# One layout for the whole kernel in place of six contiguous blocks: how tokens are dealt to partitions in a streaming weighted copy

## The chip, the cores and the metric

The kernel runs on one core of a Trainium2 chip. The metric is the device time of one execution in microseconds; for the kernel before it is 241.01 us, the median of three runs (240.65 to 241.06). A profiled execution gives the span and the trace that the rest of this text reads. Its span, 238.8 us, is a little shorter than the device time of the same execution, 240.52 us.

## The reference

Each token's row of 512 numbers is copied twice, once for each of its two experts, and each copy is multiplied by that expert's weight. The expert indices do not enter the result.

```python
batch, seq, hidden, n_experts, k = 16, 1024, 512, 8, 2
x_expanded = x[:, :, np.newaxis, :].repeat(k, axis=2)
weights = expert_weights[..., np.newaxis]
return (x_expanded * weights).astype(np.float32)
```

There are 16,384 tokens. The input x is 33.55 MB (2 KB a token), the weights are 0.13 MB (8 B a token) and the output is 67.11 MB (4 KB a token). All are float32.

## The kernel before

A tile has 128 partitions, and each partition holds a number of consecutive tokens. With 16,384 tokens a partition sees 128 tokens in all (`A_TOTAL`). The list `groups` says how they are dealt out. An inner list is one group: a stretch of the input that is contiguous in memory, 128 x T tokens for a group of T, where partition p takes T consecutive tokens of the stretch. The numbers in an inner list are the tiles into which the group is cut.

```python
TX = 24     # tokens per partition in an input tile
TO = 12     # tokens per partition in an output tile
groups = [[24], [24], [24], [24], [24], [8]]

def rows(of_all, done, T):
    return of_all[done * P : (done + T) * P, :].rearrange(
        "(p a) n -> p (a n)", a=T
    )
```

So in a group of 24 the tokens of partition p begin 24 tokens after those of partition p-1. That is 48 KB in x and 96 KB in the output.

The weights are loaded first, with one DMA for each group on SyncE's queue. In a group of 24 every partition receives a row of 24 x 2 x 4 = 192 B, in the last group one of 64 B.

```python
for at, T in weights:
    nc.sync.dma_start(out=w_tile[:, at * k : (at + T) * k], in_=rows(wf, at, T))
```

The inputs are loaded on ScalarE's queue. There are two input buffers, and a tile is loaded two tiles ahead of its use. A tile of 24 tokens is one DMA of 6 MB with 128 rows of 48 KB.

```python
def load(i):
    ...
    cols = rows(xf, done, T)[:, a0 * hidden : (a0 + n) * hidden]
    ...
        nc.scalar.dma_start(out=x_tile[lo:hi, : n * hidden], in_=cols[lo:hi, :])
```

The loop multiplies token by token. Of three products VectorE makes two and ScalarE one. After 12 tokens the output tile, again 128 rows of 48 KB, is stored on SyncE's queue. There are two output buffers.

```python
for i, (done, T, a0, n) in enumerate(tiles):
    x_tile = loaded[i]
    outr = rows(of, done, T)
    for t in range(n):
        ...                                   # a new o_tile every TO tokens
        for kk in range(k):
            c = (done + a0 + t) * k + kk
            ...                               # c % 3 == 2: nc.scalar.mul
                                              # otherwise:  nc.vector.tensor_scalar
        if (t + 1) % TO == 0 or t + 1 == n:
            at = t // TO * TO
            nc.sync.dma_start(
                out=outr[:, (a0 + at) * row : (a0 + t + 1) * row],
                in_=o_tile[:, : (t + 1 - at) * row],
            )
    load(i + 2)
```

Of the kernel before, what the change touches and what calls it, by code (L numbers as in the profile page):

```python
# [1 line left out]

# [4 lines left out]


@with_exitstack
def kernel(  # L10
    ctx: ExitStack,
    tc: tile.TileContext,
    x: bass.AP,
    expert_indices: bass.AP,
    expert_weights: bass.AP,
    out: bass.AP,
):
    nc = tc.nc

    batch, seq, hidden = x.shape  # L20
    k = expert_weights.shape[-1]
    P = nc.NUM_PARTITIONS
    ntok = batch * seq
    assert ntok % P == 0
    A_TOTAL = ntok // P

    f32 = mybir.dt.float32
    row = k * hidden
    TX = 24
    TO = 12  # L30


    groups = [[24], [24], [24], [24], [24], [8]]
    assert sum(sum(g) for g in groups) == A_TOTAL

    xf = x.rearrange("b s h -> (b s) h")
    of = out.rearrange("b s k h -> (b s) (k h)")
    wf = expert_weights.rearrange("b s k -> (b s) k")

    w_pool = ctx.enter_context(tc.tile_pool(name="w_pool", bufs=1))  # L40
    x_pool = ctx.enter_context(tc.tile_pool(name="x_pool", bufs=2))
    o_pool = ctx.enter_context(tc.tile_pool(name="o_pool", bufs=2))

    w_tile = w_pool.tile([P, A_TOTAL * k], f32)
# [6 lines that stand above are left out]
    weights = []  # L51
    for group in groups:
        weights.append((sum(n for _, n in weights), sum(group)))
    for at, T in weights:
        nc.sync.dma_start(out=w_tile[:, at * k : (at + T) * k], in_=rows(wf, at, T))

    tiles = []
    done = 0
    for group in groups:
        T = sum(group)  # L60
        a0 = 0
        for n in group:
            tiles.append((done, T, a0, n))
            a0 += n
        done += T

    loaded = []

    def load(i):
        if i >= len(tiles):  # L70
            return
        done, T, a0, n = tiles[i]
        x_tile = x_pool.tile([P, TX * hidden], f32)
        cols = rows(xf, done, T)[:, a0 * hidden : (a0 + n) * hidden]
        for lo, hi in [(0, P)]:
            nc.scalar.dma_start(out=x_tile[lo:hi, : n * hidden], in_=cols[lo:hi, :])
        loaded.append(x_tile)

    for i in range(2):
        load(i)  # L80
# [4 lines that stand above are left out]
            if t % TO == 0:  # L85
                o_tile = o_pool.tile([P, TO * row], f32)
            for kk in range(k):
                c = (done + a0 + t) * k + kk
                o = t % TO * row + kk * hidden
                if c % 3 == 2:  # L90
                    nc.scalar.mul(  # L91
                        out=o_tile[:, o : o + hidden],
                        in_=x_tile[:, t * hidden : (t + 1) * hidden],
                        mul=w_tile[:, c : c + 1],
                    )
                    continue
                nc.vector.tensor_scalar(  # L97
                    out=o_tile[:, o : o + hidden],
                    in0=x_tile[:, t * hidden : (t + 1) * hidden],
                    scalar1=w_tile[:, c : c + 1],  # L100
                    scalar2=None,
                    op0=mybir.AluOpType.mult,
# [9 lines that stand above are left out]
# [1 line left out]
_INS = ['x', 'expert_indices', 'expert_weights']  # L113
_OUTS = [((16, 1024, 2, 512), 'float32')]


# [23 lines left out]
```

## Time and profile before

| quantity | value |
|---|---|
| device time, median of three | 241.01 us |
| span of the profiled execution | 238.8 us |
| VectorE busy | 68.6 us, 171 products of 480 ns |
| ScalarE busy | 54.5 us, 85 products of 709 ns |
| moved by the DMA engines | 100.81 MB, 422 GB/s over the span |
| transfers of x | 5 of 6144 KB, 1 of 2048 KB |
| transfers of the output | 10 of 6144 KB, 1 of 4096 KB |
| transfers of weights | 5 of 24 KB, 1 of 8 KB |

The profile counts busy time of each engine in the span. A core has 16 DMA engines that work side by side; the share of a DMA queue is the time that its packets took as a share of the time of all 16. A packet is here one row of a transfer (one partition's part), or one 4 B word that reports an engine's part of a transfer as done. A wait is put down to the instruction or transfer that ended it.

### The profile page before, as it was taken

To read this page: it belongs to the slowest core of one execution; us is meant where nothing else is said; L and a number is where in the kernel's file an instruction comes from. 1 tells how busy PE (TensorE), PEld (TensorE's weight loads), DVE (VectorE), ACT (ScalarE), POOL (GpSimd) and SP (SyncE) were. 2 spreads that over 40 slices of the span, in tenths; PEclk is the share of its full clock that TensorE was granted. 3 is DMA by queue.
4 is the path that set the end of the run, shared out by engine and by line. 5 is a ranking of instruction groups with operands and counts; after the bars stand their busy time and mean duration, and the time that the engine had idled before them with its cause. 6 is when DMAs were issued, how large, how long until landed. Compare 5 with 4: busy or idle time off the path is not lost.

```text
span 238.8 us, 363 instructions
## 1 busy us (share of the span) xinstructions
DVE 68.6 (29%) x171; ACT 54.5 (23%) x86; POOL 0.2 (0%) x4
## 2 busy tenths in 40 slices
DVE  0009920000270820550054055002705506415000
ACT  0109700000350800520052043003505206213000
POOL 0000000000000000000000000000000000000000
DMA  7999999999999999999999999999989899999994
GB/s 275 462 438 413 421 375 403 477 428 403 445 461 412 413 477 412 412 477 428 412 428 461 420 412 471 428 403 436 469 379 488 384 450 461 436 395 436 439 434 209
DMA packets 3314, 100.81 MB, mean 422 GB/s; under 512 B 1136, under 2 KB 1136, under 8 KB 1136
## 3 DMA queue, kind: packets, MB, share of 16 engines
q1 hardware_dynamic: 2448, 67.24, 65.2%
q10 hardware_dynamic: 864, 33.55, 33.2%
q14 instruction: 2, 0.02, 0.0%
HBM read 33.69 MB, written 67.11 MB: 422 GB/s over the span
## 4 chain that ended last, share of the span: by engine, by line
DMA 60%; DVE 17%; issue 14%; DVEq 0%; SPq 0%
DMA out_dram<-o_tile 53%; DVE o_tile L97 17%; DMA x_tile<-in_x_dram 7%; DVEq L135 0%; DVEq L97 0%; SPq L106 0%
## 5 line engine op out<-in xcount | busy, mean ns | idle before, releaser
L97 DVE TENSOR_SCALAR o_tile<-x_tile,w_tile 128x512 f32<-128x512 f32 x171 | 68.6, 480 | 149.7 <-DMA out_dram<-o_tile 98.5
L91 ACT ACTIVATE o_tile<-x_tile,w_tile 128x512 f32<-128x512 f32 x85 | 53.2, 709 | 151.4 <-DMA out_dram<-o_tile 145.4
L91 ACT ACT_TABLE_LOAD x1 | 1.3, 1283 | 11.2 <-DMA w_tile<-in_expert_weights_dram 11.2
L124 POOL MEMSET const-bfloat16-1.0<- 128x1 bf16 x1 | 0.1, 101 | 0.0
L124 POOL MEMSET const-uint8-127<- 128x1 uint8 x1 | 0.1, 101 | 0.0
L124 POOL MEMSET const-float32-0.0<- 128x1 f32 x1 | 0.1, 98 | 0.2 <-issue 0.2
L124 POOL MEMSET const-float32-1.0<- 128x1 f32 x1 | 0.1, 98 | 0.0
## 6 DMA issues: line engine op xcount, KB each, us to landing
out_dram<-o_tile SPq DMA_DIRECT2D x10, 6144.0 KB, 35.2
x_tile<-in_x_dram ACTq DMA_DIRECT2D x5, 6144.0 KB, 33.3
out_dram<-o_tile SPq DMA_DIRECT2D x1, 4096.0 KB, 19.5
x_tile<-in_x_dram ACTq DMA_DIRECT2D x1, 2048.0 KB, 24.0
w_tile<-in_expert_weights_dram SPq DMA_DIRECT2D x5, 24.0 KB, 32.0
w_tile<-in_expert_weights_dram SPq DMA_DIRECT2D x1, 8.0 KB, 31.5
```

The source lines that it names most:

```text
L91: nc.scalar.mul(out=o_tile[:, o : o + hidden], in_=x_tile[:, t * hidden : (t + 1) * hidden], mul=w_tile[:, c : c + 1],)
L97: nc.vector.tensor_scalar(out=o_tile[:, o : o + hidden], in0=x_tile[:, t * hidden : (t + 1) * hidden], scalar1=w_tile[:, c : c + 1], scala ...
L124: nc = _bacc.Bacc("TRN2", target_bir_lowering=False, num_devices=1)
```

## The change

The six groups become one group of 128 tokens, cut into the same six tiles.

```diff
--- before.py
+++ after.py
@@ -30,7 +30,7 @@
     TO = 12
 
 
-    groups = [[24], [24], [24], [24], [24], [8]]
+    groups = [[24, 24, 24, 24, 24, 8]]
     assert sum(sum(g) for g in groups) == A_TOTAL
 
     xf = x.rearrange("b s h -> (b s) h")
```

Partition p now owns tokens 128p to 128p+127 for the whole kernel. The tiles, their sizes, the buffers, the order and the number of products stay as they are. What differs is where the rows of a transfer lie in memory. Neighbouring rows of an x tile are 128 x 2 KB = 256 KB apart, where before they followed each other without a gap at 48 KB. Neighbouring rows of an output tile are 128 x 4 KB = 512 KB apart, where before they were 96 KB apart. Each row is still one contiguous run of 48 KB (in the last tile 16 KB of x and 32 KB of output). The weights become one DMA with 128 rows of 1 KB. The change makes the code simpler: one weight load, and a fixed owner for each token.

## The prediction on record

> **What bounds the kernel now.** I first read busy times against the span, then the slices, then the DMA queues, then the waits.
>
> ```profile
> span 238.8 us, 363 instructions
> DVE 68.6 (29%) x171; ACT 54.5 (23%) x86; POOL 0.2 (0%) x4
> ...
> DMA  7999999999999999999999999999989899999994
> ...
> q1 hardware_dynamic: 2448, 67.24, 65.2%
> q10 hardware_dynamic: 864, 33.55, 33.2%
> ```
>
> The two engines that compute are idle for over 70% of the span. The DMA engines are at 9 tenths or more in all but four of the 40 slices, the first and last among those four. The queue that carries weights and outputs (q1) takes 65.2% of the 16 engines' time and the one that carries x (q10) 33.2%, together 98.4%. That is 0.984 x 238.8 = 235.0 us of work on each DMA engine, with 3.8 us left, most of it at the two ends. The waits agree:
>
> ```profile
> ACT o_tile L91 <- DMA out_dram<-o_tile: 145.4, 9, 35.5
> DVE o_tile L97 <- DMA out_dram<-o_tile: 98.5, 8, 19.0
> ...
> DVE o_tile L97 <- DMA x_tile<-in_x_dram: 18.4, 1, 18.4
> ACT L91 <- DMA w_tile<-in_expert_weights_dram: 11.2, 1, 11.2
> ACT o_tile L91 <- DMA x_tile<-in_x_dram: 6.0, 1, 6.0
> ```
>
> The columns are total wait, number of waits and longest wait. Compute waits mainly for stores to free an output buffer. A wait for weights occurs once, at 11.2 us, and ends 7 us before the first x tile lands (18.4 us), so it sets nothing. The kernel is bound by the DMA engines through nearly its whole length: a nanosecond more for each row goes straight into the time, and a faster engine elsewhere is worth nothing.
>
> **Whether the memory or the DMA engines set the pace of a row.** In the records of single packets in the trace, the shortest and the median 48 KB row both took 1815 ns, for x and for outputs, which is 27.1 GB/s for one engine and 433 GB/s for 16. Such a sharp floor says that the DMA engine sets the pace and that memory now has some room. Of the 1920 rows of 48 KB only 57 took over 1830 ns. Most of those lie in two bursts of x rows: one at the start, where the first row on each engine took about 1.8 to 2.9 us, and one 29 us into the span, just after the first store is issued, where 16 rows took 2.4 to 3.3 us. The excess of all x rows over 1815 ns is 26.5 us, or 1.7 us per engine. When engines change what they do at the same moment, memory can become the slower side even with today's addresses.
>
> **What the Trainium skill says.** "DMA: Bandwidth & Descriptors", section "Latency and other measured facts", has an entry on row pitch at large powers of two: copies between tensors in HBM, 128 partitions of 16 KiB, at a pitch of 512 KiB gave 207 GB/s in each direction, at 2 MiB 164, at 4 and 8 MiB 103, and 214 with 4 KiB of padding. It calls the cause, rows in step falling on the same HBM channels, an inference. The trace before cannot confirm it: its pitches are 48 and 96 KB, and it runs at the floor. The section "The descriptor swizzle" of the same page deals a 128-partition transfer out to the engines in runs of four partitions (0 to 3 and 32 to 35 for the first). The trace does not name the engine of a packet, so no run here shows it. "Queues, rings and completion order" says that an engine takes packets in turn from the queues that have work for it. Here the trace agrees: at the start a 192 B weight row and a 48 KB x row follow each other on alternate queues, with starts about 12 ns apart.
>
> **The change, part by part.**
>
> *Weights.* Before: 640 rows of 192 B, 15 ns each in the median, and 128 rows of 64 B at 11 ns. Their recorded sum is 9.58 + 1.41 = 10.99 us, or 0.69 us on each of 16 engines. After: 128 rows of 1 KB, 8 per engine. A 48 KB row costs 1815/48 = 37.8 ns per KB; a 192 B row took 15 ns where that rate gives 7.1, so I add 8 ns per row and estimate 46 ns. That is 8 x 46 = 0.37 us per engine. Five transfers fewer also drop five completion words of 9 ns each per engine, 0.05 us. Gain: 0.69 - 0.37 + 0.05 = 0.37 us. All of it is engine time, so it counts in full.
>
> *Start.* The first weight transfer before needed 8 rows per engine and landed at about 11 us, taking turns with x. The new one also has 8 rows per engine, each 31 ns longer, so it should land at about the same moment, well before x at 18.4 us. The SyncE queue issues one transfer instead of six (3.4 us before), off the path. I count zero.
>
> *Compute.* The index c runs over the same numbers, so the split of products is the same, at 480 and 709 ns. Zero.
>
> *Sizes, buffers, tail.* Rows, transfers and order of x and outputs are the same. The last store is again 4 MB. Zero.
>
> *Addresses.* This is the only large term and its sign can only be against the change, because rows already run at the engine's floor for nearly all of the span. Output rows, at 512 KB pitch, take 2324.6 + 155.3 = 2479.9 us, or 155.0 us per engine. X rows, at 256 KB, take 1188.1 + 78.2 = 1266.3 us, or 79.1 us per engine. The page's 214 against 207 is 3.4% more time. If it held for output rows alone, 155.0 x 0.034 = 5.3 us. For both kinds, 234.1 x 0.034 = 8.0 us. But these are loads and stores between HBM and SBUF, where only one end of a row can collide, with rows three times as long, and x has half the pitch of the page's mildest case. Reads and writes are also mixed and out of step, which spreads addresses. I take about 40% of the 5.3 us plus a little for x and starts: 2.4 us.
>
> Sum: 241.0 - 0.4 + 2.4 = 243.0 us.
>
> **The rivals.**
>
> *No penalty.* Memory has enough room, the rows stay at 1815 ns and only the weight gain is left: 241.0 - 0.4 = 240.6 us. For it: the sharp floor at 1815 ns, long contiguous rows, and rows on different engines that start up to about 1 us apart, so that they stand at different offsets. Against it: the bursts above show that memory's room is not unlimited. I give this 40%.
>
> *A mild penalty,* from a fifth of the page's 3.4% up to the whole of it on both kinds: 242 to 248.6 us. For it: the page's 512 KiB figure at a total HBM traffic (2 x 207 = 414 GB/s) very like ours (422 GB/s). Against it: the differences just named. 40%.
>
> *A heavy penalty,* from 249 us up. If engines keep in step and each has a run of four partitions, as the swizzle has it, rows in flight at once are 4 x 512 KB = 2 MB apart in the output and 1 MB in x. The page's 2 MiB figure would then be the one to use: 155.0 x (214/164 - 1) = 47 us for outputs alone, 288 us in all, more with x. For it: engines in this trace do stay within about one row of each other. Against it: the page's pitch is that of partitions, so its 512 KiB case probably contains a similar multiplication already and still lost only 3%. Rows could also collide like this for a part of the time. 18%, half of it below 262 us.
>
> *A gain of over 2%,* which needs 4.8 us. The gaps are 3.8 us and the slow x rows 1.7 us; nearly all of both would have to go, and nothing in the change aims at them. 2%.
>
> **Range and chances.** The lower end is the weight gain plus a part of the slow x rows: 241.0 - 0.4 - 0.6 = 240.0 us. The upper end, 262 us, lies above the whole mild penalty and holds the weaker half of the heavy one. The limit for slower by over 2% is 245.8 us. I put three fifths of the mild 40% below it (24%) and two fifths above (16%). So within 2% is 40 + 24 = 64%, slower is 16 + 18 = 34%, and faster keeps its 2%. The middle of the distribution is near 242.5 us, and I name the sum, 243.0 us.
>
> **What would show each step right or wrong.** Weights: one transfer with 128 rows of 1 KB near 46 ns, and q1 with 720 packets fewer (640 rows and 80 completion words). Start: first product near 18.4 us; later means that the first x tile already suffers. Compute: still 480 and 709 ns with 171 and 85 products. Addresses: the number to look at is the time of a 48 KB row, against 1815 ns, separately for x and outputs. At 1815 ns the first rival is right; up to about 1880 ns the mild one; over 2200 ns on outputs the heavy one. If only a few engines' rows are slow, the DMA share falls while others wait, and median time from issue to landing rises above 35.2 us without the median row doing so. The prediction is wrong if the time falls below 240 us, which would mean that the power-of-two pitches help, or if it exceeds 262 us.

## The result and the profile after

The changed kernel takes 242.19 us (median of six runs, 241.54 to 242.67) against 241.03 us for the kernel before (six runs, 240.65 to 241.17). The ratio is 1.0051, with a 95% interval of 1.0034 to 1.0068: slower by about half a per cent, 1.2 us. The single profiled executions are 2.2 us apart (spans of 241.0 and 238.8 us), so a trace of one execution shows the kind of the loss, and the medians its size.

This is the page of the changed kernel, the lines that answer to those of before:

```profile
span 241.0 us, 358 instructions
DVE 68.6 (28%) x171; ACT 54.5 (23%) x86; POOL 0.2 (0%) x4
...
DMA  7999999999999999999999999999999999999994
...
q1 hardware_dynamic: 1728, 67.24, 64.6%
q10 hardware_dynamic: 864, 33.55, 33.5%
...
out_dram<-o_tile SPq DMA_DIRECT2D x10, 6144.0 KB, 34.3
...
w_tile<-in_expert_weights_dram SPq DMA_DIRECT2D x1, 128.0 KB, 12.0
```

In the last two lines the final number is the median time from issue to landing in microseconds. Compute is the same to the tenth of a microsecond. The DMA engines are just as full, and q1 carries 720 packets fewer. But 64.6% + 33.5% of 241.0 us is 236.4 us of work, against 235.0 us, although the same data is moved with fewer packets. The share of q10 (x) rises while that of q1 falls: rows of x take longer. The waits of the changed kernel:

```profile
ACT o_tile L91 <- DMA out_dram<-o_tile: 147.6, 9, 32.1
DVE o_tile L97 <- DMA out_dram<-o_tile: 133.5, 9, 29.3
DVE o_tile L97 <- DMA x_tile<-in_x_dram: 18.2, 1, 18.2
ACT L91 <- DMA w_tile<-in_expert_weights_dram: 12.8, 1, 12.8
ACT o_tile L91 <- DMA x_tile<-in_x_dram: 4.1, 1, 4.1
```

The start is not worse. The weights arrive at 12.8 us rather than 11.2, still well before the first x tile, and that tile lands at 18.2 rather than 18.4 us. VectorE's wait for stores looks longer (133.5 against 98.5 us), but this is mostly book-keeping. In the kernel before, one more wait of that engine is listed under "issue", that is, with no releaser found:

```profile
DVE o_tile L97 <- issue: 32.8, 1, 32.8
```

With it the two sums are 133.5 and 131.3 us. Compute is idle in either case.

The end of the run shows a second part of the loss. These are the last stretches of before and after: stretch, its length, busy time of the three engines, clock, DMA share, GB/s.

```profile
230.00:235.00 5.00, 0.00 (x0) 0.00 (x0) 0.00 (x0) 1.00 1.05 452
235.00:239.00 4.00, 0.00 (x0) 0.00 (x0) 0.00 (x0) 1.00 0.23 98
```

```profile
230.00:235.00 5.00, 0.00 (x0) 0.00 (x0) 0.00 (x0) 1.00 1.03 446
235.00:241.00 6.00, 0.00 (x0) 0.00 (x0) 0.00 (x0) 1.00 0.39 169
```

After 235 us the mean engine still had 0.23 x 4 = 0.9 us of work before the change, and 0.39 x 6 = 2.3 us after it. A share of 0.39 over several microseconds is not 16 engines at work to the end: most are done and a few finish late. The records of single packets put numbers on both parts. An engine's last packet is the word that reports its part of the last store; times here count from the first data packet of the run, and excess is the time that 48 KB rows took beyond 1815 ns each, summed and divided by 16.

| profiled execution | mean end of the 16 engines | last end | last minus mean | excess, x | excess, output |
|---|---|---|---|---|---|
| before | 234.74 | 235.79 | 1.04 | 1.66 | 0.09 |
| after | 236.18 | 237.74 | 1.56 | 3.05 | 0.32 |

The last engine ends 1.95 us later: 1.44 us because the engines have more work on average, and 0.52 us because the work is spread less evenly. Of the first part, 1.3 us is accounted for: 1.39 + 0.23 us of longer rows, less about 0.3 us for the smaller weight packets. The median row is still 1815 ns. What has changed is how many rows stand out: 98 of 640 rows of x took over 1830 ns (41 before), and 45 of 1280 output rows (16 before). They come in bursts. The burst between 25 and 33 us of the span, where the first store meets the second load of x, grew from 0.97 to 1.59 us per engine, while the slow rows of the first 5 us fell from 0.64 to 0.36 us. New bursts of x rows stand at 41 us (0.32 us) and 57 us (0.50 us), and one of output rows at 132 us (0.21 us).

### The profile page after: what moved, and what is told of

Same layout as the page of the kernel before. It is cut to its first block, busy times and chain, and to the rows that moved or that the text cites. A ratio compares the mean times of both kernels' runs of the same rounds, so it can differ in the third digit from the quotient of the medians.

```text
span 241.0 us, 358 instructions
## 1 busy us (share of the span) xinstructions
DVE 68.6 (28%) x171; ACT 54.5 (23%) x86; POOL 0.2 (0%) x4
## 3 DMA queue, kind: packets, MB, share of 16 engines
q1 hardware_dynamic: 1728, 67.24, 64.6%
q10 hardware_dynamic: 864, 33.55, 33.5%
## 4 chain that ended last, share of the span: by engine, by line
DMA 75%; DVE 15%; issue 0%; DVEq 0%; SPq 0%
DMA out_dram<-o_tile 68%; DVE o_tile L97 15%; DMA x_tile<-in_x_dram 7%; DVEq L135 0%; DVEq L97 0%; SPq L106 0%
## 5 line engine op out<-in xcount | busy, mean ns | idle before, releaser
L97 DVE TENSOR_SCALAR o_tile<-x_tile,w_tile 128x512 f32<-128x512 f32 x171 | 68.6, 480 | 151.7 <-DMA out_dram<-o_tile 133.5
L91 ACT ACT_TABLE_LOAD x1 | 1.3, 1283 | 12.8 <-DMA w_tile<-in_expert_weights_dram 12.8
## 6 DMA issues: line engine op xcount, KB each, us to landing
out_dram<-o_tile SPq DMA_DIRECT2D x10, 6144.0 KB, 34.3
```

The costliest lines, as they stand in the source:

```text
L91: nc.scalar.mul(out=o_tile[:, o : o + hidden], in_=x_tile[:, t * hidden : (t + 1) * hidden], mul=w_tile[:, c : c + 1],)
L97: nc.vector.tensor_scalar(out=o_tile[:, o : o + hidden], in0=x_tile[:, t * hidden : (t + 1) * hidden], scalar1=w_tile[:, c : c + 1], scala ...
```

## The experiments

My theory: rows far apart at a power of two slow each other, x above all, since its excess grew most. Rivals: the output's pitch is the cause and x rows are its victims; mere spreading is enough, without a power of two; the new weight load disturbs the rows. All changes are made to the kernel before unless another is named, and each ratio is to the kernel before as it was timed beside them (240.83 us, and 241.12 us for the stores and loads alone).

**The weight load alone.**

```diff
-    for at, T in weights:
-        nc.sync.dma_start(out=w_tile[:, at * k : (at + T) * k], in_=rows(wf, at, T))
+    nc.sync.dma_start(out=w_tile, in_=rows(wf, 0, A_TOTAL))
```

> The layout of x and of the output as before; only the six weight loads become one of 128 rows of 1 KB (products then use other tokens' weights). If the weights are a small gain that the addresses outweigh, 0.3 to 0.4 us less than before (ratio 0.998 to 0.999) and few slow x rows (about 41 over 1830 ns, excess near 1.7 us per engine). If the new weight load itself disturbs the x rows, 1 us more than before, with x rows slow as in the changed kernel (98 over 1830 ns).

Measured: 240.64 us, ratio 0.9986 (0.9979 to 0.9994), a gain of 0.3 us. 30 rows of x were over 1830 ns, with 1.08 us of excess. The weight load is a small gain, and it does not disturb the rows. The gain did not come as forecast, though: in this trace the 128 weight packets took 16.7 us together, against 11.0 us for the 768 packets before. What fell is the excess of x rows, by 0.58 us per engine.

**The pitch of x alone.**

```diff
-        cols = rows(xf, done, T)[:, a0 * hidden : (a0 + n) * hidden]
+        cols = rows(xf, 0, A_TOTAL)[:, (done + a0) * hidden : (done + a0 + n) * hidden]
```

> Only x is read with rows 256 KB apart; weights are loaded and outputs are stored as before (products land in other tokens' places). If the 256 KB pitch of x is the cause, about 1.5 us more than before (ratio 1.006) and x rows with about 3 us of excess per engine. If the 512 KB pitch of the output is the cause and x rows are only its victims, as before (ratio 1.000) with 1.7 us of excess.

Measured: 241.19 us, ratio 1.0015 (1.0003 to 1.0027), excess of x rows 1.58 us. My theory in its first form falls: reading x at 256 KB makes by itself the smaller part of the loss, 0.4 us and by the interval at most 0.65 us. Nor is it nothing: 7 of its 22 runs took over 241.5 us, against 3 of 51 of the kernel before, and in its trace the last engine ended 2.02 us after the mean, where before it was 1.04 us.

**The pitch of the output alone.**

```diff
-        outr = rows(of, done, T)
+        outr = rows(of, 0, A_TOTAL)[:, done * row :]
```

> Only the output is stored with rows 512 KB apart; x and weights are loaded as before (products land in other tokens' places). If the pitch of x is the cause, as before (ratio 1.000), with 1.7 us of excess on x rows. If the output's pitch is the cause, about 1.5 us more (ratio 1.006).

Measured: 242.43 us, ratio 1.0055 (1.0038 to 1.0072). This change alone makes a loss as large as that of the whole change. Its page and the end of its run:

```profile
span 242.0 us, 363 instructions
...
q1 hardware_dynamic: 2448, 67.24, 64.7%
q10 hardware_dynamic: 864, 33.55, 33.1%
```

```profile
230.00:235.00 5.00, 0.00 (x0) 0.00 (x0) 0.00 (x0) 1.00 0.99 426
235.00:242.00 7.00, 0.00 (x0) 0.00 (x0) 0.00 (x0) 1.00 0.35 150
```

After 235 us there are 0.35 x 7 = 2.5 us of work for the mean engine, at a third of the full share. The packet records give a mean end of 236.18 us and a last end of 238.90, so 2.72 us of unevenness against 1.04 before. This was the slowest of the kernel's six runs (243.63 us), so the end shown is worse than its usual one. The excess is 2.54 us on x rows and 0.54 us on output rows. So although only the store addresses changed, the loads slow down as well, by 0.88 us of the 1.39 us seen in the changed kernel. X rows are to a large part victims, and the share of q10 in the changed kernel had pointed at the wrong transfer.

**Nearly the same spread, without the power of two.**

```diff
-    groups = [[24], [24], [24], [24], [24], [8]]
+    groups = [[24, 24, 24, 24, 24], [8]]
```

> The groups are 24 x 5 tokens and 8 tokens: rows of x 240 KB and of the output 480 KB apart in the first five tiles, nearly as far as in the changed kernel but no power of two; two weight loads. If power-of-two pitches collide, 0.3 us less than before (ratio 0.998 to 0.999), x rows as before. If it is the mere spread over all of x and the output, 1 us more than before (ratio 1.005).

Measured: 240.85 us, ratio 0.9997 (0.9989 to 1.0004). The loss is gone, though rows of the output still lie 480 KB apart. The gain of 0.3 us that I had expected from fewer weight loads is not seen either. The same for the output alone:

```diff
-        outr = rows(of, done, T)
+        outr = rows(of, 0, 120)[:, done * row :] if done < 120 else rows(of, 120, 8)
```

> As the run with the output's rows 512 KB apart, but 480 KB apart in the first ten stores and 32 KB in the last; x and weights as before (products land in other tokens' places). If the exact power of two in the output's pitch matters once loads and stores meet, the time of before (ratio 1.000, within 0.3 us). If wide spreading of stores is enough, the ratio of the 512 KB run, 1.0055.

Measured: 240.71 us, ratio 0.9998 (0.9987 to 1.0008), where 512 KB gave 1.0055. The end of its run is that of the kernel before:

```profile
230.00:235.00 5.00, 0.00 (x0) 0.00 (x0) 0.00 (x0) 1.00 1.00 433
235.00:239.00 4.00, 0.00 (x0) 0.00 (x0) 0.00 (x0) 1.00 0.29 123
```

So spreading alone is not the cause: the loss appears between 480 and 512 KB. The two kernels without it also have contiguous rows in the last store, but that is not the difference, since these 32 KB rows took 1213 ns on average in all of these traces. That 512 KB costs because it is a power of two is the nearest reading and is not shown: no larger pitch was run.

The bursts draw the same line. Leave out the first 31 us after the first packet. Then the x rows of the two kernels so far with the output at 512 KB have 1.09 and 0.94 us of excess per engine and their output rows 0.31 and 0.54 us. In the five others, the kernel before among them, x rows have 0.00 to 0.14 us and output rows 0.05 to 0.13 us.

**Stores alone and loads alone.** Two kernels make the eleven stores from one tile that is filled once; they read no input and multiply nothing. Two others make the six loads and a store of 256 KB at the end. "Far" has the layout of the changed kernel.

```diff
+    o_tile = o_pool.tile([P, TO * row], f32)
+    nc.vector.memset(o_tile, 1.0)
     for i, (done, T, a0, n) in enumerate(tiles):
-        ...
+        outr = rows(of, done, T)                           # near
+        outr = rows(of, 0, A_TOTAL)[:, done * row :]       # far
+        for at in range(0, n, TO):
+            m = min(TO, n - at)
+            nc.sync.dma_start(out=outr[:, (a0 + at) * row : (a0 + at + m) * row],
+                              in_=o_tile[:, : m * row])
```

> The eleven stores alone, from one tile filled once, with rows 96 KB apart as before; no input is read and nothing is multiplied. All theories: 155 us of rows at the floor and about 5 us of start and end, near 160 us.

> The same eleven stores with rows 512 KB apart. If stores collide among themselves in steady flow, rows are over 1815 ns throughout: 162 us or more (the mild penalty in full would be 165 us, the heavy one 200 us or more). If rows collide only where loads and stores meet, the same as with rows 96 KB apart to within 0.5 us.

> The six loads of x alone with rows 48 KB apart, into two buffers in turn; one store of 256 KB at the end, nothing multiplied. All theories: 77.5 us of rows at the floor and about 6 us of start and end, near 84 us.

> The same six loads with rows 256 KB apart. If loads at this pitch collide among themselves, 1 us or more above the loads at 48 KB, with rows over 1815 ns throughout. If the pitch of x does next to nothing by itself, within 0.5 us of them.

Measured: stores 173.04 us near (173.03 to 173.05) and 173.05 us far (173.05 to 173.09). Loads 86.02 us near and 85.60 us far, ratios 0.3568 (0.3558 to 0.3579) and 0.3552 (0.3545 to 0.3558). The stores take 13 us more than I expected, mainly because filling the tile stands ahead of them. This is the far store kernel, start, length, and what ran:

```profile
3.36 10.30 DVE L64 MEMSET o_tile<- 128x12288 f32 x1 [3.36 <-issue]
13.69 6.98 SPq L69 DMA_DIRECT2D out_dram<-o_tile  x7
```

The queues of the near store kernel and then of the far one show the same share of the same span:

```profile
span 171.3 us, 57 instructions
...
q1 hardware_dynamic: 1584, 67.11, 90.9%
```

```profile
span 171.3 us, 57 instructions
...
q1 hardware_dynamic: 1584, 67.11, 90.8%
```

At 512 KB the store rows had a median of 1820 ns, as at 96 KB, with 121 rows over 1830 ns in both. So the pitch costs nothing while only stores run, and loads at 256 KB were even 0.4 us quicker. The loss needs both directions in flight, or the stopping and starting of the whole kernel, which the store runs also lack: there the transfers queue up and wait for no buffer. These runs do not tell the two apart.

**Half the pitch.** Two groups of 64 tokens give pitches of 128 and 256 KB; the second kernel has the same tile sizes in contiguous groups.

```diff
-    groups = [[24], [24], [24], [24], [24], [8]]
+    groups = [[24, 24, 16], [24, 24, 16]]              # 128 and 256 KB
+    groups = [[24], [24], [16], [24], [24], [16]]      # contiguous
```

> Two groups of 64 tokens in tiles of 24, 24 and 16: rows of x 128 KB and of the output 256 KB apart, half the changed kernel's. To be compared with the run of the same tiles and contiguous groups. If any large power of two in the output's pitch costs, 0.5 us or more above that run. If it takes the full 512 KB, the same within 0.3 us, or a little less for two weight loads instead of six.

> Six contiguous groups of 24, 24, 16, 24, 24 and 16 tokens: the tile sizes of the run with pitches of 128 and 256 KB, with the layout of before. One store more than before (twelve). All theories: within 0.5 us of before.

Measured: 241.68 us, ratio 1.0026 (1.0009 to 1.0043), for 128 and 256 KB; 242.23 us, ratio 1.0061 (1.0046 to 1.0075), for contiguous groups. Half the pitch costs nothing against its partner and is even faster; two weight loads in place of six may be part of that. But the partner itself missed its expectation by 0.9 us, and against the kernel before, with its other tile sizes, half the pitch loses 0.6 us. So this pair does not settle whether 256 KB between output rows costs something. In the partner's trace the 256 rows of 32 KB of x took 1275 ns on average against a median of 1213, which makes 1.0 us per engine. The cause is open. It is a reminder that a kernel with no far pitch can lose as much to bursts as the changed one. A loss of about 1 us is thus no mark of the pitch by itself; the case against 512 KB rests on several kernels on each side of it.

**The changed kernel with six weight loads.**

```diff
-    groups = [[24], [24], [24], [24], [24], [8]]
+    groups = [[24, 24, 24, 24, 24, 8]]
...
-    for at, T in weights:
-        nc.sync.dma_start(out=w_tile[:, at * k : (at + T) * k], in_=rows(wf, at, T))
+    for at, T in [(0, 24), (24, 24), (48, 24), (72, 24), (96, 24), (120, 8)]:
+        cols = rows(wf, 0, A_TOTAL)[:, at * k : (at + T) * k]
+        nc.sync.dma_start(out=w_tile[:, at * k : (at + T) * k], in_=cols)
```

> The changed kernel, with its weights loaded by six transfers of 192 B and 64 B rows again (now 1 KB apart). If the parts simply add, 0.3 to 0.4 us more than the changed kernel, near 242.5 us (ratio 1.0065). If the single weight load owes its gain to a start that no longer matters here, the changed kernel's 1.005.

Measured: 243.39 us, ratio 1.0109 (1.0088 to 1.0130), more than either expectation. Against the changed kernel it loses 1.0109 - 1.0051 = 0.0058, or 1.4 us, where 0.3 to 0.4 us of weight packets had been expected (the near ends of the two intervals are 0.5 us apart, so the surplus may be small).

```profile
span 242.2 us, 363 instructions
...
q1 hardware_dynamic: 2448, 67.24, 64.7%
q10 hardware_dynamic: 864, 33.55, 33.1%
```

The packets of its six loads are no longer than before (15 ns). Its mean end is 236.68 us, 0.50 us after the changed kernel's, while its last end is 239.16 us, 1.42 us after: in these two traces most of the difference is unevenness (2.48 against 1.56 us). Past the first 31 us its rows have 1.13 us of excess (x) and 0.86 us (output), so this kernel too stands with those at 512 KB. How the transfers happen to fall in time may make the surplus; no run tests that, and the cause stays open.

This run also shows that the parts do not simply add. It has six weight loads like the kernel before, and both pitches far. The output's pitch alone cost 1.3 us and that of x 0.4 us; together, with the weight rows 1 KB apart, they cost 2.6 us (1.0109).

## Why the prediction was right, and where its steps were off

*The bound.* Right. Compute was unchanged, and the loss is DMA time and the wait for the last engine.

*Weights.* Right in size: 0.37 us was forecast. The new packets took 46 ns in the median, and in the changed kernel the recorded sum fell from 0.69 to 0.39 us per engine, with 0.04 us of completion words besides. The single load by itself gained 0.3 us too, but there the packets took longer and x rows less long, so that this agreement is partly luck. In the changed layout it was worth more, for the reason left open above.

*Start and compute.* Right. The first x tile landed at 18.2 us, and the 171 and 85 products kept their times.

*Addresses.* The sign was right. I put 2.4 us; measured are 1.6 us with one weight load (1.0051 against 0.9986) and 2.6 us with six (1.0109). For the change as made the size was too large. Parts measured one at a time seem to agree: output +1.3 us, x +0.4 us, weights -0.3 us, together 1.4 us against 1.2 us for the whole change. But by the same sum the two pitches with six weight loads should cost 1.7 us, and they cost 2.6 us, so this agreement may be luck. That 2.4 us came near is partly luck as well, since the 40% in it was chosen and not worked out. That output pitch weighs more than that of x was also the split I had made. Two assumptions in this step failed. I reckoned with a slowdown of rows in general, taken as a fraction of 3.4%. That is the step from 214 to 207 GB/s which the Trainium skill's "DMA: Bandwidth & Descriptors", section "Latency and other measured facts", has between padded copies and copies at 512 KiB. Rows in steady flow did not get slower: the median stayed at 1815 ns, stores alone showed 0.0%, and the loss sits in bursts while loads and stores share the engines. And I counted the time of the mean engine only. Followed in time, the packets of the traces before and after fall into 16 chains with 40 rows of x and 80 of the output each. With such a fixed share for each engine the last one decides, and this term was missing from the sum. In the profiled executions it grew by 0.5 us in the changed kernel and 1.7 us with the output's pitch alone; what it is on average was not measured. The page's explanation, rows in step on the same channels, is consistent with 512 against 480 KB. No run here observes a channel, so it stays an inference.

*Signs.* The number I had named to tell the rivals apart, the time of a 48 KB row, would have misled. Its median of 1815 ns was to mean that there is no penalty, and the median landing time of the 6 MB stores, which was to rise above 35.2 us if only a few engines suffer, fell to 34.3 us. The loss is in the tail of the rows, which a median does not see: x rows took 1891 ns on average (1856 before) and output rows 1819 ns (1816 before).

*The rivals.* No penalty (240.6 us) is excluded by the interval. The mild one holds by its time, just at its lower edge of 242 us, though not as rows that are slower throughout. The heavy one falls: output rows at 512 KB stayed at 1815 ns in the median, far from the 2200 ns of that rival. Which rows are on the 16 engines at one time was not measured.

## What to carry to other kernels

When the DMA engines are full, compare row times by their outliers and by the last engine's end as well as by the median: here the median did not move at all. Read the last engine's end from several executions if you can: in single traces of four kernels without a loss it came 0.98 to 1.35 us after the mean. A transfer whose rows slow down may be the victim of another one, so move one side's addresses at a time before blaming it. If a layout puts output rows 512 KB apart while loads run beside the stores, try a neighbouring count first (120 tokens and a remainder of 8 in place of 128): it kept nearly the same layout and, here, the whole loss went.

## What the runs showed of the hardware that I had not expected

The cost of a pitch depended on what else was running: 512 KB between output rows cost nothing in 155 us of stores alone (173.05 against 173.04 us) and 1.3 us in the whole kernel. The slow first rows at the start appear with loads alone too: in the near load kernel 18 rows of the first 5 us made 0.84 us of excess per engine, so neither weights nor stores are needed for them. And small choices at the start, such as six weight transfers instead of one, moved the changed kernel by more than their own packets weigh: 1.4 us by the ratios (0.5 us by the near ends of the intervals), against 0.3 us.
